# Shifting the operand tiles of a two-layer decoder trunk to a common address remainder, and one attention step by one place

## The chip, the cores and the metric

One core of one Trainium2 chip. The time is device microseconds of one execution; of several executions the median is given. The engines are named as the profile names them: PE (TensorE matmul), PEld (TensorE weight load), DVE (VectorE), ACT (ScalarE), POOL (GpSimd), SP (SyncE).

## What is computed

A decoder trunk of two layers on 256 tokens of width 2048, all in float32. Each layer is a token mixer and an MLP, each with a residual and an RMSNorm ahead of it.

```python
for i in range(2):
    h = rmsnorm(x, norm_mix[i])
    x = x + (sliding_window_sink_attention(h, ...) if i == 0 else stick_breaking_attention(h, ...))
    h = rmsnorm(x, norm_mlp[i])
    x = x + squared_relu_mlp(h, mlp_w_in[i], mlp_w_out[i])      # (relu(h @ w_in) ** 2) @ w_out, hidden 8192
return rmsnorm(x, final_norm)
```

Mixer A (layer 0) has 32 query heads and 4 key/value heads of 64, a window of 128 keys, a distance penalty per head and a learned sink in the softmax's denominator. Mixer B (layer 1) is stick-breaking attention with 32 heads. Each mixer ends in an output projection.

## The kernel before, in words

**Precision.** Every operand of a projection is held as two float32r parts, high and low. A product is three matmuls: high by high, high by low, low by high. Weights come from memory as tiles `wraw` of 1 MB (SP's queue, three buffers); for each half tile ACT copies the high part (L67) and DVE subtracts for the low part (L75), into one of five `wsplit` buffers. `WeightStream.tick` runs after every step of a projection: on even steps it may split (ACT), on odd steps it does what is left for DVE. In the query projections one half tile serves four steps, so the DVE subtraction comes at steps 1, 5, 9 and 13.

**Projections.** `proj` (L290) has the weights stationary and the activations `xg` moving: in each of 16 steps (`kt`) four matmuls, two of 256 columns and two of 512. `proj_v` (L322) has `xg` stationary and the weights moving, in the same shapes. `proj_wide` (L299), for the output projections and the second MLP matrix, has the activations (`attnT` or `h`) stationary and the weights moving: three matmuls of 512 columns for each of two token halves of a step.

**Order of work.** PE, ACT and DVE run in program order. `plan` puts a piece of work at a place, which is a number of steps from now; `between`, after each step, issues what is planned for that place and then ticks the weight stream. Each engine keeps the order in which things are issued, so moving a piece by a place moves its instructions in each engine's queue.

**Attention of mixer A.** Eight groups (L542 to L555) of four heads, in two pairs u = 0 and 1. A group projects its queries in 16 steps of `proj`. After them ACT copies half of each bank (`low`, L330), DVE adds (`t`, L332) and scales (`qf`, L352), and the result is split into `qhl` (ACT L337, DVE L340). Then, while the next group's projection runs on PE, these stages follow, at planned places:

- `scores` (places 3 and 5): PE multiplies queries and keys (L380, L382) into two banks of tag `s`; DVE adds the penalties (L486), takes maxima (L490, L491) and makes the negated maximum `nm` (L495) and `es` (L497). 
- `powers` (places 6 and 9): ACT's exponentials (L504, L507), with `nm` as bias.
- `total` (7 and 13): DVE (L511, L512). `normalise` (13 and 14): ACT (L518).
- In the group after, the `older` list: four `transposed` at places 1, 1, 7, 8 (PE L389 into one `s` bank each; ACT L337 and DVE L340 write `pTa`), and `values` at place 14 (PE L537; ACT L337 and DVE L340 write `attnT`).

The tag `s` has four banks in turn. The second scores of a group take the two banks that the two transposes of place 1 used, so they wait until DVE has read these (`pTa`, L340). The last group, n = 7, has places of its own, which run beside the output projection.

**Addresses.** The pools are stacked: `const` (`gains`, `sums`, a pad of 96 bytes per partition, `xg`, `xt`), `wpool` (`wraw`, `wsplit`), `stat` (small tiles), then one pool for the stage (`attn_a` and `attn_a_out`, `mlp0`, `attn_b`, `mlp1`). Each partition's start address, modulo 512 bytes (its rest), is for the kernel before: `xg` 0, every `wsplit` buffer 0, `h` of both MLPs 128, `attnT` of mixer B 128, `attnT` of mixer A 320. So `proj` and `proj_v` have equal rests already, and the `proj_wide` passes have not.

Of the kernel before, what the change touches and what calls it, by code (L numbers as in the profile page):

```python
# [10 lines left out]
F32 = mybir.dt.float32  # L11
# [6 lines left out]
P = 128  # L18
# [127 lines left out]
def trunk_kernel(ctx: ExitStack, tc, x, a_w_qkv, a_w_o, a_sinks, b_w_qkv, b_w_o, norm_mix, norm_mlp,  # L146
# [31 lines left out]
    specs += mlp_specs(1)  # L178

    const = ctx.enter_context(tc.tile_pool(name="const", bufs=1))  # L180
    gains = const.tile([P, 4, NDT], F32, name="gains")
    sums = const.tile([P, 2, 4], F32, name="sums")
    const.tile([P, 24], F32, name="pad")
    xg = const.tile([P, NDT, 2, S], F32R, name="xg")
    xt = [const.tile([P, D], F32, name=f"xt{tt}") for tt in range(2)]
    wpool = ctx.enter_context(tc.tile_pool(name="wpool", bufs=3))
    stat = ctx.enter_context(tc.tile_pool(name="stat", bufs=1))
# [13 lines left out]
    def plan(*stages):  # L201

        for place, stage in stages:
            while len(side) <= place:
                side.append([])
            side[place].append(stage)
# [7 lines left out]
        return psum.tile([P, 512], F32, name=tag, bufs=bufs)  # L214


    ident = stat.tile([P, P], F32, name="ident")
    make_identity(nc, ident)
    ones = stat.tile([P, P], F32, name="ones")
# [60 lines left out]
    def proj(nk, act):  # L280

        banks = two_banks()
        for kt in range(nk):
            if kt % UK == 0:
                wt = W.narrow()
            for u, cols in ((1, S), (0, 2 * S)):
                for j in range(2):
                    nc.tensor.matmul(banks[j][:, :cols], lhsT=wt[:, u, kt % UK, j * P : (j + 1) * P],  # L290
                                     rhs=act[:, kt, : cols // S, :], start=(kt == 0 and u == 1),
                                     stop=(kt == nk - 1 and u == 0), skip_group_check=True)
            between()
        return banks
# [52 lines left out]
    def scaled(tmp, banks, r, name):  # L347

        ts = [summed(tmp, b) for b in banks]
        fs = [tmp.tile([P, S], F32, name=f"{name}f", bufs=2) for _ in ts]  # L350
        for f, t in zip(fs, ts):
            nc.vector.tensor_mul(out=f, in0=t, in1=r)  # L352
        hls = [tmp.tile([P, 2, S], F32R, name=f"{name}hl", bufs=2) for _ in ts]

        def parts():
            for f, hl in zip(fs, hls):
                split(hl[:, 0, :], hl[:, 1, :], f, 0)

        plan((0, parts))
        return list(zip(fs, hls))  # L360
# [55 lines left out]

    scale = {}
    with tc.tile_pool(name="attn_a", bufs=1) as tmp, ExitStack() as second:
        k = tmp.tile([P, 2, 2, S], F32R, name="ka")
        kf = tmp.tile([P, 2, S], F32, name="kfa")  # L420
        vpad = tmp.tile([P, 2, 2, 2, 3, HD], F32R, name="vpad")
# [104 lines left out]
        def values(pTs, gp, i):  # L526

            o = bank("s", 4)
            ops = []
            for hh in range(2):  # L530
                vs = [[vpad[:, part, kt, gp, hh : hh + 2, :] for kt in range(2)] for part in range(2)]
                ps = [pTs[hh][:, part].rearrange("p n u q -> p (n u q)") for part in range(2)]
                for v, p in ((0, 0), (0, 1), (1, 0)):
                    ops += [(o, vs[v][0], ps[p][:, : 2 * S]), (o[:, S:], vs[v][1], ps[p][:, 2 * S :])]
            ops[-2:] = ops[:-3:-1]
            for n, (out, v, p) in enumerate(ops):
                nc.tensor.matmul(out, lhsT=v, rhs=p, start=(n == 0), stop=(n == len(ops) - 1))  # L537
            hi, lo = [attnT[:, gp * 8 + i : gp * 8 + i + 2, part, :].rearrange("p u (n q) -> p u n q", n=2) for part in range(2)]
            split(hi, lo, o.rearrange("p (n u q) -> p u n q", n=2, u=2), 0)

        older = None
        for n in range(8):  # L542
            gp, i = n // 4, n % 4 * 2
            qs = scaled(tmp, proj(NDT, xg), r8, "q")
            pair = [head_pair(gp, i + u, *qs[u]) for u in range(2)]
            pTs = [tmp.tile([P, 2, 3, 2, P], F32R, name="pTa", bufs=2) for _ in range(2)]
            late = [lambda u=u, hh=hh, t=pair[u][1], pTs=pTs: t(pTs, u, hh) for u in range(2) for hh in range(2)]
            late.append(lambda pTs=pTs, gp=gp, i=i: values(pTs, gp, i))
            if older:
                plan(*zip((1, 1, 7, 8, 14) if n < 7 else (0, 3, 3, 6, 12), older))  # L550
            if n < 7:
                plan(*zip((3, 6, 7, 13), pair[0][0]), *zip((5, 9, 13, 14), pair[1][0]))
            else:
                plan(*zip((3, 4, 5, 6), pair[0][0]), *zip((3, 6, 8, 11), pair[1][0]), *zip((10, 12, 13, 13, 18), late))
            older = late  # L555
# [170 lines left out]
```

## Time and profile before

| | us |
|---|---|
| median of 3 runs (lowest, highest) | 2124.79 (2124.70, 2126.79) |
| the profiled execution's own time | 2126.64 |
| its span | 2124.9 |
| PE busy in it | 2100.7 |

The order of the stages in the span, by first matmuls: mixer A's keys, values and queries to 170 us, its output projection to 274, the first MLP to 993 (two halves of an input and an output part), mixer B to 1301 and its output projection to 1399, the second MLP to the end. A row of a timeline gives start, duration, engine, line and operation, output and input tiles, and in brackets how long the engine was idle before it and what ended that.

### The profile page before, as it was taken

Reading aid. Unit: us, or ns where it says so; the run is one execution under the profiler, and the core shown is the slowest. Engines: PE = TensorE matmul, PEld = TensorE weight load, DVE = VectorE, ACT = ScalarE, POOL = GpSimd, SP = SyncE. Lnnn points to the kernel's source line nnn. Section 1 sums busy time; section 2 is a strip of 40 time slices with the busy share of each in tenths; the row PEclk is TensorE's granted clock in tenths of the full one; section 3 lists DMA queues with packets and bytes.
Section 4 is the critical chain, followed back from the end, with each engine's and each line's share of the span. In section 5 each row is a group of like instructions: output and inputs, shape, how many; then the busy total and the mean of one; then the engine's idle time right before and its main releaser. Section 6 shows DMA issues by size and latency. Waiting matters only on the chain.

```text
span 2124.9 us, 27479 instructions
## 1 busy us (share of the span) xinstructions
PE 2100.7 (99%) x10994; PEld 1764.0 (83%) x10994; DVE 1303.5 (61%) x1845; ACT 1093.2 (51%) x1771; POOL 7.4 (0%) x17
## 2 busy tenths in 40 slices
PE   8999999999999999999999999999999999999998
PEld 7888888888888888888888888888888888888886
DVE  5886566654446665455778787566664446665453
ACT  6876455553335554444555555455553334554443
POOL 0000000000000000000000000000000000000000
PEclk9999999999999999999999999999999999999999
DMA  8555856656565566555554544565665556556553
GB/s 224 134 120 119 192 185 198 192 185 196 180 196 182 182 192 198 179 178 189 168 164 154 178 160 153 184 189 188 198 192 184 194 183 193 183 183 196 197 181 116
DMA packets 340464, 380.37 MB, mean 179 GB/s; under 512 B 72624, under 2 KB 257008, under 8 KB 340208
## 3 DMA queue, kind: packets, MB, share of 16 engines
q1 hardware_dynamic: 339760, 376.50, 57.8%
q8 instruction: 86, 1.41, 0.3%
q10 hardware_dynamic: 576, 2.11, 0.2%
q14 instruction: 42, 0.34, 0.1%
HBM read 376.49 MB, written 2.10 MB: 178 GB/s over the span
## 4 chain that ended last, share of the span: by engine, by line
PE 91%; ACT 4%; DVE 3%; issue 1%; DMA 0%; SPq 0%; ACTq 0%; DVEq 0%
PE m L290 43%; PE m L299 41%; PE m L322 4%; ACT sc L504 1%; ACT sc L518 1%; ACT wsplit L67 1%; DVE wsplit L75 1%; PE s L226 1%; PE s L389 1%; PE s L380 0%; PE s L670 0%; DVE sc L486 0%; DVE mx L490 0%; DVE t L332 0%; ACT junk L242 0%
## 5 line engine op out<-in xcount | busy, mean ns | idle before, releaser
L75 DVE TENSOR_TENSOR wsplit<-wraw,wsplit 128x1024 fp32r<-128x1024 f32 x712 | 857.8, 1223 | 548.2 <-ACT wsplit L67 547.6
L67 ACT CAST wsplit<-wraw 128x1024 fp32r<-128x1024 f32 x712 | 730.9, 1048 | 600.8 <-PE m L299 450.6
L290 PE MATMUL m<-xg,wsplit 128*128 128x256 f32 (+1 forms) x5696 | 1016.6, 338 | 3.3 <-DVE wsplit L75 3.2
L290 PEld LDWEIGHTS m<-xg,wsplit 128*128 128x128 f32 x5696 | 861.9, 189 | 125.1 <-DVE wsplit L75 3.6
L299 PE MATMUL m<-wsplit,h 128*128 128x512 f32 x3072 | 717.5, 395 | 0.0
L299 PEld LDWEIGHTS m<-wsplit,h 128*128 128x128 f32 x3072 | 577.6, 188 | 134.6
L299 PE MATMUL m<-wsplit,attnT 128*128 128x512 f32 x768 | 188.9, 401 | 0.0
L299 PEld LDWEIGHTS m<-wsplit,attnT 128*128 128x128 f32 x768 | 142.6, 189 | 32.0 <-issue 0.2
L340 DVE TENSOR_TENSOR h<-hsq,h 128x256 fp32r<-128x256 f32 x128 | 54.4, 425 | 118.0 <-ACT h L337 118.0
L330 ACT COPY low<-m 128x256 f32<-128x256 f32 x178 | 63.5, 371 | 122.7 <-PE m L290 122.6
L575 ACT ACTIVATE hsq<-t 128x256 f32<-128x256 f32 x128 | 53.5, 418 | 126.5 <-DVE t L573 126.5
L332 DVE TENSOR_TENSOR t<-m,low 128x256 f32<-128x256 f32 x178 | 72.9, 420 | 62.4 <-ACT low L330 62.3
L322 PE MATMUL m<-wsplit,xg 128*128 128x256 f32 (+1 forms) x576 | 110.8, 343 | 0.0
L322 PEld LDWEIGHTS m<-wsplit,xg 128*128 128x128 f32 x576 | 85.1, 189 | 11.4
L573 DVE SCALAR_TENSOR_TENSOR t<-t,rbc 128x256 f32<-128x256 f32 x128 | 54.4, 425 | 4.4
L337 ACT CAST h<-hsq 128x256 fp32r<-128x256 f32 x128 | 52.0, 406 | 4.1
L228 ACT ACTIVATE xg<-s,gains 128x256 fp32r<-128x256 f32 x64 | 29.0, 475 | 33.1 <-PE s L226 32.9
L231 DVE SCALAR_TENSOR_TENSOR xg<-s,gains,xg 128x256 fp32r<-128x256 f32 x64 | 29.4, 480 | 24.6 <-ACT xg L228 24.6
L365 DVE TENSOR_TENSOR xt<-m,xt 128x512 f32<-128x512 f32 x46 | 29.9, 683 | 17.2 <-PE m L299 17.2
L504 ACT ACTIVATE sc<-sc,nm 128x256 f32<-128x256 f32 x64 | 28.4, 447 | 21.4 <-DVE nm L495 21.4
L242 ACT ACTIVATE junk<-xt 128x512 f32<-128x512 f32 x40 | 25.1, 628 | 24.8 <-DVE xt L365 13.1
L653 DVE TENSOR_TENSOR_SCAN rest<-keep 128x256 f32<-128x256 f32 x64 | 35.2, 550 | 0.0
(106 smaller groups left out, 643.7 us busy)
## 6 DMA issues: line engine op xcount, KB each, us to landing
wraw<-in_mlp_w_in_dram SPq DMA_DIRECT2D x128, 1024.0 KB, 5.7
wraw<-in_mlp_w_out_dram SPq DMA_DIRECT2D x128, 1024.0 KB, 5.0
wraw<-in_b_w_qkv_dram SPq DMA_DIRECT2D x48, 1024.0 KB, 5.0
wraw<-in_a_w_qkv_dram SPq DMA_DIRECT2D x64, 256.0 KB, 4.0
wraw<-in_a_w_o_dram SPq DMA_DIRECT2D x32, 512.0 KB, 7.0
wraw<-in_b_w_o_dram SPq DMA_DIRECT2D x16, 1024.0 KB, 5.0
wraw<-in_a_w_qkv_dram SPq DMA_DIRECT2D x3, 1024.0 KB, 10.3
xt<-in_x_dram SPq DMA_DIRECT2D x4, 256.0 KB, 5.2
```

The source lines that it names most:

```text
L67: self.nc.scalar.copy(out=wt[:, 0], in_=raw)
L75: self.nc.vector.tensor_tensor(out=wt[:, 1], in0=raw, in1=wt[:, 0].bitcast(F32), op=ALU.subtract)
L290: nc.tensor.matmul(banks[j][:, :cols], lhsT=wt[:, u, kt % UK, j * P : (j + 1) * P], rhs=act[:, kt, : cols // S, :], start=(kt == 0 and u = ...
L299: nc.tensor.matmul(banks[tt], lhsT=act[:, kt, a, tt * P : (tt + 1) * P], rhs=wt[:, w, kt % 2, :], start=(first and n == 0), stop=(last and ...
L322: nc.tensor.matmul(banks[tt][:, :cols], lhsT=act[:, kt, u, tt * P : (tt + 1) * P], rhs=wt[:, : cols // S, kt % UK, :], start=(kt == 0 and ...
L330: nc.scalar.copy(out=low, in_=b[:, S:])
L332: nc.vector.tensor_add(out=t, in0=b[:, :S], in1=low)
L337: nc.scalar.copy(out=hi, in_=src)
L340: nc.vector.tensor_tensor(out=lo, in0=src, in1=hi.bitcast(F32), op=ALU.subtract)
L504: nc.scalar.activation(out=sc[:, hh, cols], in_=sc[:, hh, cols], func=AF.Exp, bias=nm[:, hh, blk : blk + 1], scale=1.0, accum_out=den[:, h ...
L573: nc.vector.scalar_tensor_tensor(out=t, in0=t, scalar=0.0, in1=scale["row"], op0=ALU.max, op1=ALU.mult)
L575: nc.scalar.activation(out=sq, in_=t, func=AF.Square)
```

## The change

A 96-byte pad in `const` stands ahead of `gains` and `sums` in place of behind them, a pad of 384 bytes opens `stat`, a pad of 320 bytes opens `attn_a`, and in groups 0 to 6 of mixer A the second pair's `scores` and `powers` stand at places 6 and 10 in place of 5 and 9.

```diff
     const = ctx.enter_context(tc.tile_pool(name="const", bufs=1))
+    const.tile([P, 24], F32, name="pad")
     gains = const.tile([P, 4, NDT], F32, name="gains")
     sums = const.tile([P, 2, 4], F32, name="sums")
-    const.tile([P, 24], F32, name="pad")
     xg = const.tile([P, NDT, 2, S], F32R, name="xg")
...
+    stat.tile([P, 96], F32, name="pad")
     ident = stat.tile([P, P], F32, name="ident")
...
     with tc.tile_pool(name="attn_a", bufs=1) as tmp, ExitStack() as second:
+        tmp.tile([P, 80], F32, name="pad")
         k = tmp.tile([P, 2, 2, S], F32R, name="ka")
...
             if n < 7:
-                plan(*zip((3, 6, 7, 13), pair[0][0]), *zip((5, 9, 13, 14), pair[1][0]))
+                plan(*zip((3, 6, 7, 13), pair[0][0]), *zip((6, 10, 13, 14), pair[1][0]))
```

## Rows read from the trace of the kernel before

**Rows 1.** The page: span, engines' busy time, and the chain by engine.
```profile
span 2124.9 us, 27479 instructions
...
PE 2100.7 (99%) x10994; PEld 1764.0 (83%) x10994; DVE 1303.5 (61%) x1845; ACT 1093.2 (51%) x1771; POOL 7.4 (0%) x17
...
PE 91%; ACT 4%; DVE 3%; issue 1%; DMA 0%; SPq 0%; ACTq 0%; DVEq 0%
```

**Rows 2.** By line: count, ns min/median/max, first and last start (us), shapes.
```profile
L290 PE MATMUL m<-xg,wsplit x1024: 274/338/398, 633.2 to 811.3; 128*128 128x256 f32 x86, 128*128 128x512 f32 x85
...
L299 PE MATMUL m<-wsplit,h x768: 389/393/404, 454.7 to 632.9; 128*128 128x512 f32 x192
...
L299 PE MATMUL m<-wsplit,attnT x87: 392/398/477, 1335.5 to 1355.6; 128*128 128x512 f32 x87
...
L299 PE MATMUL m<-wsplit,attnT x87: 393/398/478, 210.2 to 230.3; 128*128 128x512 f32 x87
...
L322 PE MATMUL m<-wsplit,xg x64: 274/377/398, 992.9 to 1005.2; 128*128 128x256 f32 x32, 128*128 128x512 f32 x32
```

**Rows 3.** Waits in the stretch 50 to 171 us: us in total, times, longest.
```profile
PEld s L380 <- DVE pTa L340: 5.7, 12, 0.7
```

**Rows 4.** Timeline of one group of mixer A (n = 3), 100 to 120 us.
```profile
100.30 1.50 ACT L518 ACTIVATE sc<-sc,den 128x256 f32<-128x256 f32 x4
...
101.70 0.63 ACT L330 COPY low<-m 128x256 f32<-128x256 f32 x2
...
104.93 1.23 DVE L75 TENSOR_TENSOR wsplit<-wraw,wsplit 128x1024 fp32r<-128x1024 f32 x1 [0.52 <-ACT wsplit L67]
...
106.08 1.02 DVE L340 TENSOR_TENSOR pTa<-s,pTa 128x384 fp32r<-128x384 f32 x2
...
106.68 1.09 PE L380 MATMUL s<-ka,qhl 64*128 64x256 f32 x6 [0.23 <-DVE pTa L340]
...
109.23 0.16 DVE L495 SCALAR_TENSOR_TENSOR nm<-mx,nsinks 128x4 f32<-128x4 f32 x1
109.43 0.51 ACT L504 ACTIVATE sc<-sc,nm 128x256 f32<-128x256 f32 x1 [2.83 <-DVE nm L495]
...
111.74 0.17 DVE L495 SCALAR_TENSOR_TENSOR nm<-mx,nsinks 128x4 f32<-128x4 f32 x1
...
112.15 1.23 DVE L75 TENSOR_TENSOR wsplit<-wraw,wsplit 128x1024 fp32r<-128x1024 f32 x1
112.98 0.51 ACT L504 ACTIVATE sc<-sc,nm 128x256 f32<-128x256 f32 x1
...
115.78 1.50 ACT L518 ACTIVATE sc<-sc,den 128x256 f32<-128x256 f32 x4
...
117.27 0.59 ACT L337 CAST attnT<-s 128x512 fp32r<-128x512 f32 x1
```

**Rows 5.** Timeline of the first group (n = 0), 58 to 69 us.
```profile
60.27 1.03 ACT L67 CAST wsplit<-wraw 128x1024 fp32r<-128x1024 f32 x1
...
60.70 0.16 DVE L495 SCALAR_TENSOR_TENSOR nm<-mx,nsinks 128x4 f32<-128x4 f32 x1
...
61.20 0.51 ACT L504 ACTIVATE sc<-sc,nm 128x256 f32<-128x256 f32 x1
...
64.01 2.87 ACT L518 ACTIVATE sc<-sc,den 128x256 f32<-128x256 f32 x8
...
66.79 0.61 ACT L330 COPY low<-m 128x256 f32<-128x256 f32 x2
```

**Rows 6.** Timeline of the last group's start (n = 7).
```profile
171.50 0.63 ACT L330 COPY low<-m 128x256 f32<-128x256 f32 x2
...
174.77 0.62 PE L380 MATMUL s<-ka,qhl 64*128 64x256 f32 x5 [0.39 <-DVE pTa L340]
```

**Rows 7.** Stretches: PE, PEld, DVE, ACT, POOL busy (count), granted clock, DMA share, GB/s.
```profile
177.00:180.00 3.00, 3.00 (x12) 2.30 (x11) 2.86 (x7) 2.03 (x10) 0.00 (x0) 0.50 0.00 0
...
183.00:186.00 3.00, 3.00 (x16) 2.42 (x16) 0.77 (x3) 3.00 (x12) 0.00 (x0) 1.00 0.40 119
```

## The prediction

> **What bounds the kernel now.** I read the page first. PE is busy for 2100.7 of 2124.9 us, and 91% of the chain that ended last is PE's [rows 1]: time can come from PE's pace inside the projections, or from the little that it waits. The change touches both, so the views by line come next (the pace), then the waits and the timeline of mixer A's groups (the waits).
>
> **The pace, by rest.** Count the intervals between first and last start [rows 2]. `proj` (L290), whose operands have equal rests already, runs 1024 matmuls from 633.2 to 811.3: 178.1 us over 1023 intervals. The wide pass over `h` (L299), rests 128 and 0, runs 768 from 454.7 to 632.9: 178.2 us over 767, 232.3 ns each. Both stream the same 393,216 columns (1024 x 384 and 768 x 512), one with equal rests and one without, and differ by 0.1 us. The same line shows two paces in undisturbed stretches: 232.3 ns, and 20.1 us / 86 = 233.7 ns, the latter for mixer B's `attnT` (rest 128) and for mixer A's (rest 320) alike. The starts are given to 0.1 us, so these 86 intervals carry an error of about 1 ns. The step is some 1 ns and does not follow the rest: at rest 128 both occur.
>
> **The waits.** In the groups of mixer A the scores (L380) wait for DVE's reads of the two transposes' banks: 5.7 us in 12 waits, two in each of six groups [rows 3]. In the timeline the second scores come at 106.68, when DVE is in the `pTa` instructions of 106.08, and the six matmuls take 1.09 us [rows 4]. This is the wait that the second edit steps around.
>
> But what sets a group's length? The low copies of n = 1 and n = 7 start at 66.79 and 171.50 [rows 5, 6]: six groups in 104.71 us, 17.45 each. Follow ACT and DVE through one of them [rows 4]. ACT waits 2.83 us for `nm` until 109.43, and then has no pause: neighbours overlap by 0.10 us in the rows, as 100.30 + 1.50 = 101.80 against a low copy at 101.70. After that low copy DVE adds, scales and splits, subtracts a weight's low part at 104.93, reads the transposes at 106.08, does the first scores and gives `nm` at 109.39, 0.04 us before ACT starts again. That is a closed ring of ACT and DVE alone. PE enters it at one point: `attnT` starts at 117.27, where its predecessor ends at 117.28, so it lacks the usual overlap of 0.10 us, which it lost waiting for `values`. Without PE the ring would take 17.35 us. **PE waits in these groups because the ring is the longer one**, by about as much as PE waits.
>
> **The change, part by part.**
>
> *Pads.* Moving the pad in `const` changes `gains` and `sums` alone; `xg` stays. The stage pools move by 384 bytes and mixer A's tiles by 704, so `h` and both `attnT` come to rest 0, as the weights have. No instruction is added. 3072 matmuls over `h` and 768 over `attnT` are concerned. What they cost at equal rests no row shows for this form; the nearest are `proj` (178.1 against 178.2 us for the same columns) and the two paces. If all 3840 ran at the better one, at most some 750 that are now at the other would gain 1 ns, 0.8 us. If all fell to the other, some 2800 would lose 1 ns, 2.8 us. I take 0, since the longest rows, 178.1 and 178.2, agree. Small tiles in `stat` and in the attention pools get other rests; the `wsplit` and `wraw` tiles, on which DVE and ACT spend most, do not move. I put 0 on that too. As a bound: if the DVE instructions of the ring, about half of its 17.45 us, changed by 1%, the ring would change by 0.09 us, 0.5 us in six groups, either way.
>
> *Second scores at place 6, on PE.* A place is four matmuls of `proj`: 178.1 / 1023 x 4 = 0.70 us. PE then reaches the second scores 0.70 us later in its own order and waits that much less for the banks. If PE set the pace this would give 0.70 us in each of six groups. It does not: the query parts of the next group come when the ring brings them, so the first scores of the next group wait instead (they wait already when n = 1 and a little later on). Late next is `qhl`, not `pTa`. The earlier finish of `values` gives the ring back its 0.10 us.
>
> *The same on DVE.* At step 5 DVE has the second scores and behind them the weight's low part: 111.74 is the second `nm`, 112.15 the L75 [rows 4]. After the change they swap: L75 of 1.23 us goes first (its high part is long done), and the second `nm` comes 1.15 us later (1.23 less the 0.08 us by which a DVE instruction starts before the end of the one ahead: 104.93 + 1.23 = 106.16 against 106.08). What was behind both, `total` and the next `pTa`, keeps its time. The weights' low part is earlier, which nobody waits for.
>
> *The same on ACT.* The second `powers` need that `nm`. In a steady group they start at 112.98, and `nm` is ready at 111.91, a slack of 1.07 us. At 111.91 + 1.15 + 0.04 = 113.10 they start 0.12 us late, and everything in the ring behind them with them. With the 0.10 us from `values` that is +0.02 us a group, 6 x 0.02 = 0.1 us. In the first group there are no transposes between the two `powers`, and the slack is small: `nm` is ready at 60.86 and `powers` start at 61.20, straight behind a weight's high part (60.27 + 1.03 = 61.30) [rows 5]. After the change they can start at 60.86 + 1.15 + 0.04 = 62.05, 0.85 us later. From there ACT has no pause up to the low copy at 66.79 (64.01 + 2.87 = 66.88), so the ring of n = 1 starts 0.85 us late. No SP or POOL work is issued in these stages but a weight load behind L75, which comes earlier.
>
> *The end of the stage.* The last group keeps its places; its scores wait for `pTa` at 174.77 [rows 6], ring time again, so it passes the delay on.
>
> **Sum.** Pads 0; first group +0.85; six groups +0.1; together +1.0 us. The profiled execution took 2126.64 us (span 2124.9 and 1.7 around it), so 2127.6 in its terms; it lies 1.85 above the median, and on the median of 2124.79 the sum is 2125.8 us. Bounds: pads -0.8 to +2.8, small tiles -0.5 to +0.5, groups 0 to +1.5. One more unknown is the clock. After the waits of the last group the granted clock falls to 0.50, 1.2 GHz, once: 12 matmuls in 177 to 180 us against 16 in 183 to 186 [rows 7], about 1 us lost. PE's waits move, so such a dip may vanish or come twice: 1 us either way.
>
> **Rivals.**
>
> *The wait was PE's after all.* If the ring follows PE, the 0.70 us come out in each of six groups and the first group's delay is swallowed: -4.2 us, 2120.6. For it: 5.7 us of waits for just these banks, and `attnT` lacking its overlap. Against: ACT runs without a pause from `nm` to the low copy, which does not ask PE. Chance 0.12.
>
> *Equal rests put the wide passes on a slower pace.* The stationary load and the moving stream would start on the same 512-byte phase, and the pace lock a step lower than either seen. For it: two paces exist, and the cause of the step is not in the rows. Against: `proj` has equal rests and no such loss. Price: 2.8 us to bring all to 233.7 ns and one more step of 1 ns on 3840, 3.8 us; with +1.0 that is +7.6, 2132.4. It decides from 3.3 us, about 0.9 ns on each. Chance 0.11.
>
> *Equal rests free the stream.* A 512-column matmul at 2.4 GHz (granted clock 1.00 in rows 7) is 213.3 ns, and the wide pass takes 232.3. If a quarter of this excess were two reads colliding, 4.75 ns on 3840 would give -18.2 us, 2107.6 with the rest of the sum. Against: `proj`, with equal rests, shows the whole excess (178.1 us for 393,216 columns; 163.8 at 2.4 GHz). Chance 0.07.
>
> The Trainium skill, TensorE: Matmul & The Clock Gate, section "Back-to-back issue gap", gives N / 2.4 + 2.5 ns as the isolated warm gap, 215.8 ns for 512 columns. By that page, and if equal rests brought the wide passes to it, an estimate of 16.5 ns on 3840 matmuls would be -63 us; the trace does not agree for `proj`, whose rests are equal and whose columns cost as much as the others'.
>
> **How the numbers follow.** Forecast 0.68, first rival 0.12, second 0.11, third 0.07, the rest 0.02 on either side. About 0.2%, 4.2 us, is what a measurement of this kernel can tell from no change: below 2120.5 is faster, above 2129.0 slower. The first rival lies on the lower border and I give half of it to faster: 0.06 + 0.07 + 0.01 = 0.14. Slower is the second rival and the other remainder, 0.12. Same 0.74. The forecast's own bounds reach from 2123 to 2130; with the first rival the range is 2120.0 to 2130.0, leaving out 0.2 (second and third rival, remainder).
>
> **What would show it.** Right: in the first group a gap of about 0.8 us on ACT between L67 and the second L504, released by `nm`; low copies of n = 1 and n = 7 still 104.7 to 104.9 us apart, all 0.9 us later; second scores without a wait and first scores waiting about 0.9 us for `qhl`; `proj_wide` parts of 178 us as before. Wrong: groups of 16.8 us, or a wide part under 177.5 or over 179.5 us.

## The result, and the profile after

The changed kernel takes 2105.96 us (2105.31 to 2106.32, four runs) against 2125.79 for the kernel before on the same chips: a ratio of 0.9906, 95% interval 0.9889 to 0.9923. It is 19.8 us faster, outside the range of 2120.0 to 2130.0.

The page of the changed kernel: span, engines, and its costliest PE groups (busy us, mean ns). Lines moved by one or two: L291 is `proj`, L300 `proj_wide`.

```profile
span 2104.4 us, 27478 instructions
...
PE 2077.8 (99%) x10994; PEld 1760.6 (84%) x10994; DVE 1303.8 (62%) x1845; ACT 1094.5 (52%) x1771; POOL 7.4 (0%) x17
...
L291 PE MATMUL m<-xg,wsplit 128*128 128x256 f32 (+1 forms) x5696 | 1016.5, 338 | 3.3 <-DVE wsplit L75 2.8
...
L300 PE MATMUL m<-wsplit,h 128*128 128x512 f32 x3072 | 699.9, 389 | 0.0
...
L300 PE MATMUL m<-wsplit,attnT 128*128 128x512 f32 x768 | 184.6, 395 | 0.0
```

Against [rows 1] the span lost 20.5 us and PE's busy time 22.9 us, while DVE's and ACT's rose by 0.3 and 1.3 us. PE did the same matmuls in less time. By line (count, ns min/median/max, first and last start), in the stretches of [rows 2] and in one without other work in mixer A's output projection:

```profile
L300 PE MATMUL m<-wsplit,h x768: 389/389/395, 453.3 to 627.1; 128*128 128x512 f32 x192
...
L291 PE MATMUL m<-xg,wsplit x1024: 274/338/398, 627.3 to 805.5; 128*128 128x256 f32 x86, 128*128 128x512 f32 x85
...
L300 PE MATMUL m<-wsplit,attnT x85: 389/389/393, 210.8 to 229.9; 128*128 128x512 f32 x85
```

Starts are given to 0.1 us, so a part's length is good to 0.1 us and the pace of its 767 intervals to 0.2 ns. The part over `h` fell from 178.2 to 173.8 us, 226.6 ns an interval in place of 232.3 [rows 2]. Mixer A's `attnT` went from some 233 to 19.1 / 84 = 227.4 ns. `proj` is as it was, 178.2 us in place of 178.1. The four `h` parts give 4.4 us each, 17.6 us, and the two output projections 1.3 and 1.8 us: 20.7 us, the whole gain and a little more.

The groups of mixer A went the other way. The timeline of the first group (start, duration, ...), and the low copy that begins the next:

```profile
57.42 0.51 ACT L506 ACTIVATE sc<-sc,nm 128x256 f32<-128x256 f32 x1 [1.36 <-DVE nm L497]
...
59.28 1.04 ACT L67 CAST wsplit<-wraw 128x1024 fp32r<-128x1024 f32 x1
...
61.00 0.16 DVE L497 SCALAR_TENSOR_TENSOR nm<-mx,nsinks 128x4 f32<-128x4 f32 x1
...
61.20 0.51 ACT L506 ACTIVATE sc<-sc,nm 128x256 f32<-128x256 f32 x1 [0.87 <-DVE nm L497]
...
66.79 0.62 ACT L331 COPY low<-m 128x256 f32<-128x256 f32 x2
```

ACT stands idle for 0.87 us ahead of the second exponentials and waits for `nm`; before, it went straight on from the weight's high part [rows 5]. The low copy still comes at 66.79, as before, because in this execution the query projection began about 1 us earlier (first matmul at 39.1 us, against 40.1). A steady group, and the low copy of n = 7:

```profile
103.89 0.96 PE L381 MATMUL s<-ka,qhl 64*128 64x256 f32 x6 [0.55 <-ACT qhl L338]
...
107.30 0.69 PE L381 MATMUL s<-ka,qhl 64*128 64x256 f32 x6
...
109.65 0.51 ACT L506 ACTIVATE sc<-sc,nm 128x256 f32<-128x256 f32 x1 [2.83 <-DVE nm L497]
...
109.86 1.23 DVE L75 TENSOR_TENSOR wsplit<-wraw,wsplit 128x1024 fp32r<-128x1024 f32 x1
...
113.23 0.17 DVE L497 SCALAR_TENSOR_TENSOR nm<-mx,nsinks 128x4 f32<-128x4 f32 x1
...
113.43 0.51 ACT L506 ACTIVATE sc<-sc,nm 128x256 f32<-128x256 f32 x1
...
116.23 1.49 ACT L520 ACTIVATE sc<-sc,den 128x256 f32<-128x256 f32 x4
...
117.63 0.56 ACT L338 CAST attnT<-s 128x512 fp32r<-128x512 f32 x1
...
172.11 0.62 ACT L331 COPY low<-m 128x256 f32<-128x256 f32 x2
```

The second scores (107.30) wait for nothing any more, and the first ones (103.89) wait longer, for `qhl`. `attnT` at 117.63 has its overlap of 0.09 us with the instruction ahead (116.23 + 1.49) again. Still the six groups from 66.79 to 172.11 take 17.55 us each, against 17.45 before [rows 5, 6].

### The profile page after: what moved, and what is told of

Its sections match the earlier page's. It is cut to its first block, busy times and chain, and to the rows that moved or that the text cites. A ratio compares the mean times of both kernels' runs of the same rounds, so it can differ in the third digit from the quotient of the medians.

```text
span 2104.4 us, 27478 instructions
## 1 busy us (share of the span) xinstructions
PE 2077.8 (99%) x10994; PEld 1760.6 (84%) x10994; DVE 1303.8 (62%) x1845; ACT 1094.5 (52%) x1771; POOL 7.4 (0%) x17
## 4 chain that ended last, share of the span: by engine, by line
PE 91%; DVE 4%; ACT 3%; DMA 1%; issue 1%; SPq 0%; ACTq 0%; DVEq 0%
PE m L291 43%; PE m L300 41%; PE m L323 5%; DVE wsplit L75 1%; DMA wraw<-in_a_w_qkv_dram 1%; ACT sc L520 1%; ACT wsplit L67 1%; ACT sc L506 1%; PE s L390 1%; PE s L227 0%; DVE sc L488 0%; PE s L381 0%; DVE mx L492 0%; PE s L672 0%; DVE t L333 0%
## 5 line engine op out<-in xcount | busy, mean ns | idle before, releaser
L75 DVE TENSOR_TENSOR wsplit<-wraw,wsplit 128x1024 fp32r<-128x1024 f32 x712 | 857.8, 1223 | 531.2 <-ACT wsplit L67 530.8
L291 PE MATMUL m<-xg,wsplit 128*128 128x256 f32 (+1 forms) x5696 | 1016.5, 338 | 3.3 <-DVE wsplit L75 2.8
L291 PEld LDWEIGHTS m<-xg,wsplit 128*128 128x128 f32 x5696 | 861.5, 188 | 125.5 <-DVE wsplit L75 3.2
L300 PE MATMUL m<-wsplit,h 128*128 128x512 f32 x3072 | 699.9, 389 | 0.0
L300 PEld LDWEIGHTS m<-wsplit,h 128*128 128x128 f32 x3072 | 575.7, 188 | 119.0
L300 PE MATMUL m<-wsplit,attnT 128*128 128x512 f32 x768 | 184.6, 395 | 0.0
L300 PEld LDWEIGHTS m<-wsplit,attnT 128*128 128x128 f32 x768 | 142.2, 189 | 28.2 <-issue 0.2
```

Of the source, the lines that this page charges most:

```text
L75: self.nc.vector.tensor_tensor(out=wt[:, 1], in0=raw, in1=wt[:, 0].bitcast(F32), op=ALU.subtract)
L300: nc.tensor.matmul(banks[tt], lhsT=act[:, kt, a, tt * P : (tt + 1) * P], rhs=wt[:, w, kt % 2, :], start=(first and n == 0), stop=(last and ...
```

## The experiments

Each kernel is compared with the kernel before on the same chip. A part of `proj` or of `h` is counted here from first to last start, which is 0.2 us less than in the expectations. *Difference* is the start address of the stationary tile less that of the moving one, modulo 256.

### Which edit did it

Pads alone:

```diff
-                plan(*zip((3, 6, 7, 13), pair[0][0]), *zip((6, 10, 13, 14), pair[1][0]))
+                plan(*zip((3, 6, 7, 13), pair[0][0]), *zip((5, 9, 13, 14), pair[1][0]))
```

> The change without its second edit: pads only, second scores and powers back at places 5 and 9. Theory (the pads gave the gain and the moved step cost 1.5 us): about 2104.5 us, wide passes over h 174.1 us each as in the changed kernel (226.7 ns a matmul), the first group's gap on ACT ahead of the second powers gone. Rival (the moved step gave part of the gain, 0.7 us in each of six groups): about 2110 us.

Measured: 2103.71 us (2103.61 to 2105.14), ratio 0.9902 (0.9887 to 0.9917). By line, and the low copies of n = 1 and n = 7 in the timeline:

```profile
L300 PE MATMUL m<-wsplit,h x768: 389/389/395, 450.7 to 624.6; 128*128 128x512 f32 x192
...
66.11 0.62 ACT L331 COPY low<-m 128x256 f32<-128x256 f32 x2
...
170.84 0.63 ACT L331 COPY low<-m 128x256 f32<-128x256 f32 x2
```

The pads give the whole gain, and more than the whole change does: a part of `h` takes 173.9 us, and the groups are back at 104.73 / 6 = 17.46 us. Some of the difference between the two is a fall of the clock that this execution lacks (see below, on why the prediction was wrong).

The places alone, in the kernel before:

```diff
-                plan(*zip((3, 6, 7, 13), pair[0][0]), *zip((5, 9, 13, 14), pair[1][0]))
+                plan(*zip((3, 6, 7, 13), pair[0][0]), *zip((6, 10, 13, 14), pair[1][0]))
```

> The kernel before with the second edit alone: no pads moved or added, second scores and powers at places 6 and 10. Theory: 1 to 1.5 us slower than before (0.85 us from the first group, 0.1 us from each of six more), so about 2127 us, the low copies of n = 1 and n = 7 about 105.3 us apart in place of 104.7. Rival (PE set the groups' pace): 4.2 us faster, about 2121.6 us, groups of 16.75 us.

Measured: 2126.51 us against 2125.03, ratio 1.0008 (0.9998 to 1.0017). The timeline:

```profile
61.20 0.51 ACT L504 ACTIVATE sc<-sc,nm 128x256 f32<-128x256 f32 x1 [0.87 <-DVE nm L495]
...
66.79 0.62 ACT L330 COPY low<-m 128x256 f32<-128x256 f32 x2
...
107.32 0.68 PE L380 MATMUL s<-ka,qhl 64*128 64x256 f32 x6
...
172.15 0.61 ACT L330 COPY low<-m 128x256 f32<-128x256 f32 x2
```

The same gap of 0.87 us, second scores (107.32) without a wait, and groups of 105.36 / 6 = 17.56 us. The step costs about 1.5 us by the medians (0.87 + 6 x 0.10 = 1.5 by the trace); the interval of the ratio just includes no change. The rival, 2121.6 us and groups of 16.75 us, falls.

### Does proj care about addresses

```diff
     const = ctx.enter_context(tc.tile_pool(name="const", bufs=1))
-    const.tile([P, 24], F32, name="pad")
     gains = const.tile([P, 4, NDT], F32, name="gains")
...
     xt = [const.tile([P, D], F32, name=f"xt{tt}") for tt in range(2)]
+    const.tile([P, 24], F32, name="pad")
     wpool = ctx.enter_context(tc.tile_pool(name="wpool", bufs=3))
```

> The changed kernel with its 96-byte pad behind xt in place of ahead of gains: xg and xt go to rest 416, all else stays. proj (5696 matmuls) and proj_v (576) then have unequal rests, the wide passes equal ones. Theory 1 (unequal rests cost 5.7 ns on every matmul of a projection, and proj gained from equal rests before the change already): about 36 us slower, 2142 us, a proj part of 1024 matmuls 184.2 us in place of 178.3. Theory 2 (only a stationary tile that starts off a multiple of 512 bytes costs): proj unchanged, proj_v 3 us slower at most, about 2108 us. Theory 3 (in proj the mix of 256 and 512 columns hides it): no change, 2106 us.

Measured: 2114.77 us, ratio 0.9952 (0.9938 to 0.9967), 8.8 us over the changed kernel. By line:

```profile
L291 PE MATMUL m<-xg,wsplit x1024: 279/338/397, 628.1 to 807.9; 128*128 128x256 f32 x86, 128*128 128x512 f32 x85
```

A part of `proj` takes 179.8 us in place of 178.2, so `proj` depends on the addresses too, but by some 1.6 us where theory 1 wanted 5.9 (184.2 less 178.3). Theories 2 and 3 had no change in `proj` and fall as well. The wide passes, whose addresses did not move, kept their 173.9 us. So a difference costs each form something of its own, and the next runs measured how much.

### The pace as a function of the difference

One kernel holds several differences, one for each stage. These kernels ran once each, so their totals say little; but the length of a part repeats: one of `h` at a difference of 0 takes 173.8 or 173.9 us in every kernel here. First the changed kernel with more pads ahead of `h`, `later` and `k`:

```diff
-        tmp.tile([P, 80], F32, name="pad")
+        tmp.tile([P, 128], F32, name="pad")
         k = tmp.tile([P, 2, 2, S], F32R, name="ka")
...
+            tmp.tile([P, 8 if layer == 0 else 64], F32, name="pad")
             h = tmp.tile([P, 32, 2, S], F32R, name="h")
...
+        tmp.tile([P, 16], F32, name="pad")
         later = tmp.tile([P, 2, P], F32, name="later")
```

> The changed kernel with other rests of the stationary tiles, one in each stage, wsplit at 0: attnT of mixer A at 192, h of the first MLP at 32, attnT of mixer B at 64, h of the second MLP at 256. Theory (the rests have to be equal modulo 512): all four stages back at 232 to 233.5 ns a matmul, h parts of 178.4 us, about 2126 us. Rival (a smaller modulus): the second MLP, at 256, stays at 226.7 ns (174.1 us a part); if the modulus is 64, mixer A and mixer B stay there too, and if it is 32, all do.

Measured: 2117.55 us. By line, `h` of the first and second MLP (rests 32 and 256), then a stretch of mixer A's `attnT` (192):

```profile
L300 PE MATMUL m<-wsplit,h x768: 392/395/397, 452.9 to 631.9; 128*128 128x512 f32 x192
...
L300 PE MATMUL m<-wsplit,h x768: 389/389/389, 1578.8 to 1752.6; 128*128 128x512 f32 x192
...
L300 PE MATMUL m<-wsplit,attnT x85: 388/392/397, 210.0 to 229.2; 128*128 128x512 f32 x85
```

At 256 the pace is that of equal rests (173.8 us): the period is 256 bytes, or a part of it; 32 (179.0 us, 233.4 ns), 64 (mixer B, 98.3 us for its pass) and, in the kernel before, 128 are slow, so it is no smaller power of two. At 192 mixer A runs at 19.2 / 84 = 228.6 ns (good to 1 ns), a value between, which no theory had.

The next four start from pads only, with a pad of B bytes between `xt` and `wpool`, which moves the weights away from `xg`, so that the difference in `proj` is B (in their rows L292 is `proj`, L301 `proj_wide`). The first moves weights, `h` and `attnT` together to 128:

```diff
     xt = [const.tile([P, D], F32, name=f"xt{tt}") for tt in range(2)]
+    const.tile([P, 32], F32, name="padw")
...
-    stat.tile([P, 96], F32, name="pad")
+    stat.tile([P, 32], F32, name="pad")
...
-        tmp.tile([P, 80], F32, name="pad")
+        tmp.tile([P, 16], F32, name="pad")
```

> Pads only, with every wsplit buffer, h and both attnT at rest 128 modulo 256 and xg at 0. Theory (the difference of the two rests counts, modulo 256): wide passes as with both at 0, 174.1 us a part of h; proj, now 128 apart, between its 178.35 us at equal rests and the 180.05 us it took 96 apart. Rival (the tile's own start on a boundary counts, whatever the other does): wide passes back at 178.4 us a part, about 2125 us.

Measured: 2103.89 us.

```profile
L301 PE MATMUL m<-wsplit,h x768: 387/389/397, 450.9 to 624.8; 128*128 128x512 f32 x192
...
L292 PE MATMUL m<-xg,wsplit x1024: 274/337/398, 625.0 to 803.1; 128*128 128x256 f32 x86, 128*128 128x512 f32 x85
```

`h` keeps its 173.9 us off every 256-byte boundary, so the tile's own start is not what counts; the difference is. The rival falls. `proj` at 128 happens to take what it takes at 0, 178.1 us against 178.2.

The second has B = 64, the smaller pad in `stat` as in the first, one of 8 floats in `attn_a` (which sets mixer A to 224), and shifts for the others:

```diff
+    const.tile([P, 16], F32, name="padw")
...
+            shift = 24 if layer == 0 else 56
+            if shift:
+                tmp.tile([P, shift], F32, name="pad")
             h = tmp.tile([P, 32, 2, S], F32R, name="h")
...
+        tmp.tile([P, 40], F32, name="pad")
         later = tmp.tile([P, 2, P], F32, name="later")
```

> Pads only, with the weights 64 bytes further than xg, and the stationary tile ahead of the weights by 224 (attnT of mixer A), 96 (h of the first MLP), 160 (attnT of mixer B) and 224 (h of the second MLP), modulo 256. Theory (the pace is a function of that difference alone, 226.7 ns at 0 and 232 to 233.5 at 32, 64 and 128, 229 at 192): 96 near 233, 160 between 229 and 233, 224 between 226.7 and 229. Rival (any difference but 0 costs the same 5.7 ns, and the 229 was something else): all four at 232 to 233.5. For proj no sign is forecast; a part of 1024 matmuls took 178.35 us at 0 and 180.05 at 96.

Measured: 2126.00 us. `h` of the first MLP, and `proj`:

```profile
L301 PE MATMUL m<-wsplit,h x768: 391/397/400, 453.2 to 632.8; 128*128 128x512 f32 x192
...
L292 PE MATMUL m<-xg,wsplit x1024: 276/336/398, 633.1 to 810.4; 128*128 128x256 f32 x86, 128*128 128x512 f32 x85
```

96 gives 179.6 us, the slowest of all (234.2 ns). 224 gave 178.9 us (233.2 ns) where the theory wanted less, and mixer B's pass at 160 took 98.4 us, as slow as at 64: of these values all but 96, which is slower still, fit the rival, one price for any difference but 0; the next run's 240 does not. `proj` gained 0.8 or 0.9 us a part at 64.

The third and the fourth take smaller steps, by a slice: `h` is allocated a little larger and begins some floats into it. In the third, pads of 48 and 8 floats put mixer A at 128 and mixer B at 32; in the fourth, pads of 56 and 24 put them at 160 and 96.

```diff
+    const.tile([P, 48], F32, name="padw")
...
-            h = tmp.tile([P, 32, 2, S], F32R, name="h")
+            fine = 4 if layer == 0 else 60
+            h = tmp.tile([P, 64 * S + fine], F32R, name="h")[:, fine:].rearrange("p (k a s) -> p k a s", k=32, a=2)
```

> Pads only, with the weights 192 bytes further than xg, and the stationary tile ahead of the weights by 128 (attnT of mixer A), 16 (h of the first MLP), 32 (attnT of mixer B) and 240 (h of the second MLP). Theory (a function of the difference): 128 and 32 as in the stages where they were seen, 232.4 and 233.3 ns; 240 not far from 226.7; 16 tells whether the step from 0 to 32 is sharp. Rival (each stage has its own pace): mixer A and mixer B keep the paces that they had at 192 and 64, 229 and 233.3.

Measured: 2107.17 us. A stretch of mixer A's `attnT` at 128, `h` at 16, `proj` at 192, `h` at 240:

```profile
L301 PE MATMUL m<-wsplit,attnT x84: 390/393/404, 208.3 to 227.6; 128*128 128x512 f32 x84
...
L301 PE MATMUL m<-wsplit,h x768: 394/396/398, 450.4 to 629.4; 128*128 128x512 f32 x192
...
L292 PE MATMUL m<-xg,wsplit x1024: 276/336/397, 629.6 to 806.1; 128*128 128x256 f32 x86, 128*128 128x512 f32 x85
...
L301 PE MATMUL m<-wsplit,h x768: 389/389/402, 1570.0 to 1743.9; 128*128 128x512 f32 x192
```

16 bytes ahead costs the full step (179.0 us), 16 behind nothing (173.9). Mixer A, 228.6 ns at 192, runs at 19.3 / 83 = 232.5 ns at 128, so a stage has no pace of its own and the rival falls; mixer B took 98.3 us for its wide pass at 32 as at 64, which decides nothing. `proj` at 192 takes 176.5 us, 1.7 less than in the changed kernel.

The fourth has B = 224 and `fine` 1 and 2, four and eight bytes.

> Pads only, with the weights 224 bytes further than xg, and the stationary tile ahead of the weights by 160 (attnT of mixer A), 4 (h of the first MLP), 96 (attnT of mixer B) and 8 (h of the second MLP). Theory (collisions of two reads that step through the same addresses): at 4 and 8 bytes the two still move together and stay within 1 ns of 226.7. Rival (exact equality counts): 4 and 8 are at 232 to 233.5 like any other difference.

Measured: 2120.24 us. `h` at 4 bytes and at 8:

```profile
L301 PE MATMUL m<-wsplit,h x768: 388/392/399, 451.5 to 629.7; 128*128 128x512 f32 x192
...
L301 PE MATMUL m<-wsplit,h x768: 387/392/397, 1576.2 to 1753.1; 128*128 128x512 f32 x192
```

One float apart takes 178.2 us (232.3 ns), two floats 176.9 (230.6). The theory of two reads that still move together within a few bytes fails; the low point is narrow on this side. The rival had 4 right and 8 wrong.

Three more, of the same edit, filled the gaps: B = 160, 192, 160, `fine` 12 and 20, 28 and 36, 44 and 52, mixer B's `attnT` 62, 59 and 50 floats into its tile (differences of 248, 236 and 200), and in the last two `xg` four floats into its own tile, which makes the differences of `proj` 160, 208 and 176.

> Pads only, stationary ahead of moving by 160 in proj, 48 in the wide passes over the first MLP's h, 80 in those over the second's, 248 (8 bytes behind) in those over mixer B's attnT, 0 in mixer A's. Theory (a function of the difference modulo 256, flat at 232 to 234.3 ns from 4 to 160, low at 240 and 0): 48 and 80 at 233 to 234 ns, parts of h of 179 to 180 us; 248, between two low points, at 227. proj at 160 is new: its known parts are 178.35 (0), 177.51 (64), 180.05 (96), 178.39 (128), 176.66 (192) and 177.51 us (224); a value between 176.7 and 178.4. Rival (low only where the two starts are equal to within a 16-byte step up): 248 at 230 or more.

> Pads only, stationary ahead of moving by 208 in proj, 112 in the wide passes over the first MLP's h, 144 in those over the second's, 236 (20 bytes behind) over mixer B's attnT, 0 over mixer A's. Theory: 112 and 144 at 232 to 234 ns, 236 just below the low point at 240, so between 227 and 233; proj at 208 between its values at 192 and 224, 176.6 to 177.5 us a part, or lower if the low point of proj lies between the two.

> Pads only, stationary ahead of moving by 176 in proj, 176 in the wide passes over the first MLP's h, 208 in those over the second's, 200 over mixer B's attnT, 0 over mixer A's. Theory (160 gave 233.3, 192 gave 228.9, 224 gave 233.3): 176 and 208 between 229 and 233.3, 200 near 229; proj at 176 176.7 us or more. Rival (a row of narrow low points at some multiples of 16): one of 176, 200 and 208 at 226.7 or lower.

Measured: 2129.59, 2128.88 and 2127.41 us, where the one run of the kernel before beside them took 2124.57. Mixer B's wide pass took 98.3 us at 248, so the theory fails there and its rival holds (at 227 ns it would be the 96.5 us of pads only); it took 97.9 at 236 and 97.5 at 200. `proj` and mixer B's pass (248) in the first of these kernels, `proj` and `h` (176) in the third:

```profile
L292 PE MATMUL m<-xg,wsplit x1024: 276/336/399, 631.2 to 810.1; 128*128 128x256 f32 x86, 128*128 128x512 f32 x85
...
L301 PE MATMUL m<-wsplit,attnT x384: 388/396/498, 1302.7 to 1401.0; 128*128 128x512 f32 x192
...
L292 PE MATMUL m<-xg,wsplit x1024: 278/338/398, 629.7 to 809.8; 128*128 128x256 f32 x86, 128*128 128x512 f32 x85
...
L301 PE MATMUL m<-wsplit,h x768: 387/392/398, 453.1 to 629.5; 128*128 128x512 f32 x192
```

`proj` missed two forecasts: 178.9 us at 160 (176.7 to 178.4 was expected) and 179.0 at 208 (176.6 to 177.5 or lower); at 176 it is the slowest seen, 180.1. `h` at 80 took 177.9, where 179 to 180 was expected. The rival of the third run, more narrow low points at multiples of 16, falls: none of 176, 200 and 208 is low. Together, in us for 393,216 columns:

| difference | 0 | 4 | 8 | 16 | 32 | 48 | 64 | 80 | 96 | 112 | 128 | 144 | 160 | 176 | 192 | 208 | 224 | 240 |
|---|---|---|---|---|---|---|---|---|---|---|---|---|---|---|---|---|---|---|
| `h`, wide | 173.8 | 178.2 | 176.9 | 179.0 | 179.0 | 178.9 | | 177.9 | 179.6 | 179.0 | 178.2 | 179.0 | | 176.4 | | 177.8 | 178.9 | 173.9 |
| `proj` | 178.2 | | | | | | 177.3 | | 179.8 | | 178.1 | | 178.9 | 180.1 | 176.5 | 179.0 | 177.3 | |

### Each form at its low point

The pads-only kernel with B = 192, and `h` and `attnT` level with the weights:

```diff
     xt = [const.tile([P, D], F32, name=f"xt{tt}") for tt in range(2)]
+    const.tile([P, 48], F32, name="padw")
...
-    stat.tile([P, 96], F32, name="pad")
+    stat.tile([P, 32], F32, name="pad")
...
-        tmp.tile([P, 80], F32, name="pad")
+        tmp.tile([P, 16], F32, name="pad")
```

> Pads only, with the stationary tile 192 bytes ahead of the moving one in proj and level with it in all wide passes (modulo 256), places 5 and 9 kept: the low point of each form as measured. Theory (the stages add): from the 2103.7 us of pads only, 1.69 us less in each of four proj parts, 1.6 in mixer B and 0.2 in mixer A's queries, 8.6 in all: about 2095 us, parts of proj 176.7 us and of h 174.1. Rival (a stage's gain is lost to the next one's waits): 2100 us or more.

Measured: 2095.37 us (2095.01 to 2095.83) against 2124.45, ratio 0.9863 (0.9847 to 0.988). The page's span, and by line:

```profile
span 2093.2 us, 27479 instructions
...
L301 PE MATMUL m<-wsplit,h x768: 387/389/397, 448.5 to 622.4; 128*128 128x512 f32 x192
...
L292 PE MATMUL m<-xg,wsplit x1024: 276/336/397, 622.6 to 799.1; 128*128 128x256 f32 x86, 128*128 128x512 f32 x85
```

The stages add, as expected (about 2095 us was): 29.1 us under the kernel before, 10.6 under the changed one. Both forms are at their low points at once.

## Why the prediction was wrong, point by point

- **The step that failed is the price of the pads**: "I take 0, since the longest rows, 178.1 and 178.2, agree." The rows were right and the inference was not. It took `proj`, with equal rests, as a sample of what a wide pass does at equal rests. The table shows two separate curves: at a difference of 0 the wide pass is at its lowest, 173.8 us, while `proj` stands in the middle of its own range of 176.5 to 180.1. That `proj` at 0 agreed with the wide pass at 128 was a coincidence of two points on two curves. The sign of being wrong that the prediction set, a wide part under 177.5 us, came in all four parts. No row of before had a wide pass at a difference of 0, so the honest bounds were those of an unseen case; the bounds I gave, -0.8 to +2.8 us, came only from the two paces that were seen.
- **The third rival was the case.** "Equal rests free the stream" had the cause, equal rests making the wide passes faster, and nearly the size: 4.75 ns on 3840 matmuls, -18.2 us, where 5.7 ns and -20.7 us came. The size was luck, since the quarter in it was a guess, and that two reads collide is not shown. I gave it 0.07 because of the same comparison with `proj`.
- **"The step does not follow the rest"** was right for what it saw. The differences of before, 64 and 128, lie on the high part of the curve, and there paces of 232.4 and 233.3 ns occur; that says nothing about 0. The 233.7 ns of the prediction holds one longer interval of 316 ns at the head of its stretch, behind other matmuls; without it the stretch of mixer B runs at 233.3. The upper bound of the pads should have counted the 3072 matmuls over `h`, 3.1 us, and not some 2800.
- **The ring of ACT and DVE is borne out.** The first rival, that PE set the groups' pace, falls: the second scores lost their wait and no group became shorter, neither in the changed kernel nor with the places alone. The first group's delay was put at 0.85 us and the gap on ACT measured 0.87; that all low copies would come 0.9 us later was not seen (0.0 and 0.6 us), since the earlier start hides it. The wait passed to the first scores and to `qhl`, as forecast.
- **The steady groups were mis-sized**: +0.02 us each was forecast, 0.10 measured. The second exponentials start 113.43 - 109.65 = 3.78 us after the first, 0.23 more than 112.98 - 109.43 [rows 4], where I had 0.12 more. The L75 that went ahead began 0.05 us after the `es` before it (109.65 + 0.16, to 109.86), not 0.08 before its end as the other did. So the places cost 1.5 us and not 1.0.
- The clock was left open by 1 us either way. Around the last group's scores it fell to 1.2 GHz once in the changed kernel too, as in [rows 7], and in the run of pads only it did not. In the 3 us ahead, 174 to 177, PE was busy for 1.97 us in the kernel before, 1.37 in the changed one and 2.24 in pads only. The stretch from 177 to 180 us, of the changed kernel and then of pads only (PE, PEld, DVE, ACT, POOL busy, granted clock, DMA share, GB/s):

```profile
177.00:180.00 3.00, 2.98 (x13) 2.29 (x13) 2.83 (x8) 1.42 (x7) 0.00 (x0) 0.54 0.00 0
```

```profile
177.00:180.00 3.00, 3.00 (x16) 2.43 (x16) 2.80 (x10) 2.68 (x10) 0.00 (x0) 1.00 0.00 0
```

13 matmuls against 16, some 0.7 us in this stretch alone; beside the 1.5 us of the places it accounts for most of the 2.25 us between the medians of the two (2105.96 and 2103.71), and an exact split was not worked out.

The Trainium skill, TensorE: Matmul & The Clock Gate, section "Step-by-step: what each phase is for", says that loading the next tile's weights takes no SBUF read bandwidth from the running matmul, because the two reads have ports of their own. That rule alone gives no reason why the pads should change anything. With the operands moved and no instruction added, the runs show 173.8 to 179.6 us for the same wide pass, so the pace cannot be taken from that rule; that the two reads are what collides, against it, is not shown.

What the two tiles compete for was not settled. That the load of the next stationary tile and the stream of the moving one hinder each other fits the run with all three tiles moved to 128 (the difference counts, the place does not), but each matmul brings its own load, and no kernel was run without them. The recorded loads do not settle it: none is longer than 188 ns at a difference of 0, some take 192 at 96 and 128, and at 32, where the pass is as slow, none is longer than 188 either.

## What to carry to other kernels

When PE is 99% busy, the start addresses of stationary and moving tiles can be a variable of their own, as they were here: sweep the difference in 16- or 32-byte steps within 256 bytes, one value for each stage of one run, and do it separately for each form of matmul. A price read from another form at the "same" setting is no price. And before a wait on the critical engine is removed, look for the ring that causes it: if two other engines close a loop without that engine, the wait only moves.

## What the runs showed that I had not expected

The pace of a 512-column matmul depends on where its operands lie, between 226.6 and 234.2 ns an interval, with period 256 bytes where it was tried (0 and 256 give 173.8 us). The low points are narrow: level and 16 bytes behind cost nothing, 4 bytes ahead cost 5.7 ns on every matmul, and 8 bytes behind, between the two, the wide pass of mixer B was slow (98.3 us against 96.5 with both level in the pads-only run). In `proj`, with its mixed 256 and 512 columns, the same addresses move a part by 2% and have their low point elsewhere, at 192.
